# Reordering the first transfers of an eight-core decoder block, and moving the norm's scale from the multiply into the shift

## The chip, the cores and the metric

The kernel runs on all eight cores of one Trainium2 chip. Each core handles one sequence of the batch, and the cores exchange nothing. The metric is device time in microseconds (us) of the slowest core. Cores 0 to 3 are one die, 4 to 7 the other, and I call 0/1, 2/3, 4/5 and 6/7 pairs.

Most executions agree within a few tenths of a per cent. Some fall into a slow state: the cores of a whole die run at a lower clock, and the time is longer. All comparisons below use fast runs only.

## The reference, cut to what matters

```python
mod = silu(c) @ w_mod + b_mod                   # per sequence: shifts sh, scales sc, gates gt
h = rmsnorm(x, g1) * (1 + sc1) + sh1            # x: 4096 x 1024 per core, float32
x = x + 0.5 * gt1 * swiglu_ffn(h, w1_in, w1_out)
h = rmsnorm(x, gm) * (1 + sc2) + sh2            # mixing: convolution heads and a recurrence
x = x + gt2 * mix(h)
h = rmsnorm(x, g2) * (1 + sc3) + sh3
x = x + 0.5 * gt3 * swiglu_ffn(h, w2_in, w2_out)
y = rmsnorm(x, gf) * (1 + f_scale) + f_shift
```

Nothing can be multiplied until the scale `sc1` and the shift `sh1` exist, and each is a product of the conditioning vector with 4 MB of float32 weights.

## The kernel before

The program is built as a list of operations with dependences and priorities. A small scheduler in the builder then simulates the engines with assumed durations and fixes the order on each of them: the tensor engine (PE), the vector engine (DVE), the scalar engine (ACT), and two issuers of transfers, SP and POOL. Two facts matter later: an engine's order is static, and the assumed duration of a transfer is shorter than what it takes in a busy stretch (2.7 us assumed for a cast of weights, 9.5 to 13.0 measured for the first four in before).

```python
def load_slab(nm, r, cast, prio=None, after=()):     # 10 slots of 512 KB
    b = new(sl, f"{nm}{r}")
    if cast:                                         # first use: float32 in HBM -> bf16, issued by POOL
        dma("PL", lambda: b.ap, lambda: src, D_CAST, ..., slab=True, prio=prio, after=after)
        dma("SP", lambda: d.ap, lambda: b.ap, ...)   # and the bf16 copy is written back for later tiles
...
def mods(m, afters):                                 # one modulation vector: 8 slabs of 512 KB
    for q in range(8):
        b = new(sl, f"mod{m + q}")
        dma("SP", ..., slab=True, prio=P.prio)
        A("DVE", 1.3, f, [crow], [b, modr[m]], after=(afters[q],))   # multiply and sum, 1.2 us
...
P.prio = -24; mods(M_SC1, [None] * 8); gs_op(M_SC1, V_G1)   # scale: gs = g * (1 + sc)
P.prio = -20; mods(M_SH1, [None] * 8)                       # shift
...
def norm(xs, msc, msh, after=(), prio=None):
    r = stats(xs, after, prio)                       # squares (ACT), sums (DVE, PE), rsqrt (ACT)
    for f in range(8):
        stt(t_, xs[f], gs[msc], r, mult, mult)       # DVE: (x * gs) * r
        act(b, t_, Identity, bias=modv[msh])         # ACT: + shift, to bf16; DVE may take it
...
for pi, tiles in enumerate(pairs):                   # two tiles of 512 tokens share each weight slab
    xss = [load_x(x_dr, t, prio=(-22 if t == 0 else -15) if pi == 0 else lp, after=prev_in[...]) for t in tiles]
    hbs = [norm(xs, M_SC1, M_SH1, after=(last_in,), prio=300) for xs in xss]
    for j in range(FC):                              # 22 slabs of the input weights
        slab = load_slab("w1i", j, pi == 0)
        ops = ffn_in(slab, hbs, hids, j)             # both tiles: gate and up, 16 matmuls each
        if pi == 0 and j == 1:
            gt_anchor = ops[-1]
        if j >= 3:
            next_in.append(ops[-1])                  # the next pair's x loads follow these, one by one
    if pi == 0:
        mods(M_GT1, [gt_anchor] * 8)                 # the gate GT1: 8 more slabs
    ...                                              # output weights, then the next pair
```

The next pair's tiles 2 and 3 matter below: the chunks of their x load beside slabs 3 to 18 of the first pair.

## Time and profile before

| | before |
|---|---|
| timed runs | 2420.52, 2420.62 us, and 2465.01 (slow) |
| profiled execution, slowest core | 2431.0 us (core 1), 2432.64 us in all |
| PE busy | 2317.3 us, 95% of the span |
| first weight matmul | 66.40 us |

The busy time by stretches of the profiled core of before. Columns: the stretch, its length, busy us of each engine (with the number of instructions), the granted PE clock, the share of time in which the 16 DMA engines were busy, and what they moved.

```profile
core 1: us, PE busy (x) PEld busy (x) DVE busy (x) ACT busy (x) POOL busy (x), PEclk, DMA share, GB/s
0.00:45.00 45.00, 1.17 (x2) 0.21 (x2) 19.47 (x44) 14.06 (x20) 1.94 (x7) 1.00 0.96 259
45.00:70.00 25.00, 4.77 (x11) 1.56 (x12) 19.66 (x34) 11.16 (x17) 1.05 (x2) 1.00 1.02 286
70.00:90.00 20.00, 20.00 (x91) 8.96 (x90) 11.03 (x19) 6.69 (x10) 2.11 (x4) 1.00 0.54 168
90.00:200.00 110.00, 110.00 (x512) 49.88 (x510) 25.73 (x40) 19.12 (x32) 10.55 (x20) 1.00 1.03 209
200.00:300.00 100.00, 94.36 (x428) 42.19 (x427) 34.88 (x52) 24.82 (x40) 10.75 (x20) 0.97 0.70 199
...
```

Before 70 us PE does almost nothing while the DMA engines are full. From 70 to 90 us they are half idle, and from 90 to 200 us both PE and DMA are full.

The timeline of PE in before, ahead of its first weights and at tile 3. The brackets hold the idle time before a piece and what ended it.

```profile
49.24 0.59 PE L443 MATMUL ps<-sb_h,sb_ones 128*128 128x512 bf16 x1 [3.51 <-DVE sb_h L423]
66.40 4.00 PE L443 MATMUL ps<-sb_h,sb_slab 128*128 128x512 bf16 x9 [16.57 <-ACT sb_h L401]
...
227.77 0.38 PE L443 MATMUL ps<-sb_h,sb_ones 128*128 128x512 bf16 x1
233.78 0.59 PE L443 MATMUL ps<-sb_h,sb_ones 128*128 128x512 bf16 x1 [5.63 <-DVE sb_h L423]
```

Matmuls with `sb_ones` sum the squares for the norm; those with `sb_slab` are weight matmuls. The 5.63 us at 228 us is PE waiting for the squares of tile 3, whose x had not landed.

The two operations of the norm among the groups by form (busy us, mean ns of one):

```profile
L419 DVE SCALAR_TENSOR_TENSOR sb_c<-sb_c,sb_gs 128x512 f32<-128x512 f32 x256 | 173.5, 746 | 32.6 <-ACT sb_c L401 32.5
...
L401 ACT ACTIVATE sb_h<-sb_c,sb_modv 128x512 bf16<-128x512 f32 x160 | 105.1, 716 | 20.5 <-DVE sb_c L419 10.3 <-DVE sb_modv L423 9.6 <-issue 0.2
```

### The profile page before, as it was taken

How to read it: one execution, taken by the hardware profiler on the slowest of the kernel's cores; microseconds unless marked ns; L12 is line 12 of the kernel's file. 1: busy time of each engine (PE TensorE's matmuls, PEld its weight loads, DVE VectorE, ACT ScalarE, POOL GpSimd, SP SyncE). 2: the span in 40 equal slices, each digit the busy share in tenths (PEclk: the TensorE clock that was granted, in tenths of full speed). 3: DMA queues.
4: the chain of work that ended last, by engine and by line, in shares of the span. 5: the costliest groups of instructions: out<-in, count | busy, mean ns of one | idle time of the engine just before them, and what ended most of it. 6: DMA issues, size and time to landing. Idle time of an engine off the chain costs nothing.

```text
span 2431.0 us, 34520 instructions; the slowest of 8 cores (2409.5 to 2431.0 us)
## 1 busy us (share of the span) xinstructions
PE 2317.3 (95%) x11168; PEld 1093.3 (45%) x11168; DVE 1180.9 (49%) x1975; ACT 920.8 (38%) x1394; POOL 115.1 (5%) x221
## 2 busy tenths in 40 slices
PE   0999999999999999999899999999999999999996
PEld 0444444444444445454354454454454454454442
DVE  4513233523352337676285385484484574573322
ACT  2313111401130115556264364364364464473312
POOL 0100100010000000000000000000000000000000
PEclk9999999999999999999999999999999999999998
DMA  9899589768966755565976555555555555555551
GB/s 266 201 210 242 161 203 231 181 193 206 222 188 178 191 160 196 168 216 163 223 190 220 190 176 189 185 179 189 176 179 185 191 182 182 186 179 189 166 181 61
DMA packets 131711, 460.32 MB, mean 189 GB/s; under 512 B 16048, under 2 KB 16176, under 8 KB 130864
## 3 DMA queue, kind: packets, MB, share of 16 engines
q1 hardware_dynamic: 113184, 378.15, 48.8%
q0 software_dynamic: 18352, 79.97, 16.4%
q8 instruction: 94, 1.54, 0.3%
q14 instruction: 81, 0.66, 0.1%
HBM read 446.78 MB, written 79.69 MB: 217 GB/s over the span
## 4 chain that ended last, share of the span: by engine, by line
PE 84%; DMA 5%; SPq 4%; ACT 3%; issue 2%; DVE 2%; ACTq 0%; DVEq 0%; POOL 0%; POOLq 0%
PE ps L443 84%; SPq L450 4%; ACT sb_c L401 2%; DMA sb_c<-xmid 2%; DMA sb_c<-x 1%; DMA sb_slab<-wmod 1%; DMA sb_slab<-w2o 1%; DVE sb_c L734 0%; DVE sb_c L409 0%; ACT L401 0%; DVE sb_h L423 0%; ACT sb_h L401 0%; DVE sb_c L423 0%; DVE sb_c L419 0%; DVE sb_c L429 0%
## 5 line engine op out<-in xcount | busy, mean ns | idle before, releaser
L443 PE MATMUL ps<-sb_h,sb_slab 128*128 128x512 bf16 x9984 | 2176.7, 380 | 16.6 <-ACT sb_h L401 16.6
L443 PEld LDWEIGHTS ps<-sb_h,sb_slab 128*128 128x128 bf16 x9984 | 978.7, 98 | 1196.5 <-issue 28.0
L423 DVE TENSOR_TENSOR sb_h<-ps,sb_c 128x512 bf16<-128x512 f32 x352 | 240.7, 690 | 770.0 <-PE ps L443 728.3
L401 ACT ACTIVATE sb_c<-ps 128x512 f32<-128x512 f32 x400 | 237.7, 596 | 891.8 <-PE ps L443 891.4
L401 ACT ACTIVATE sb_c<-sb_c 128x512 f32<-128x512 f32 x332 | 204.4, 627 | 294.3 <-DVE sb_c L419 194.9
L401 ACT ACT_TABLE_LOAD x102 | 130.9, 1283 | 219.3 <-PE ps L443 195.9
L419 DVE SCALAR_TENSOR_TENSOR sb_c<-ps,sb_gth,sb_c 128x512 f32<-128x512 f32 x128 | 94.9, 749 | 216.6 <-PE ps L443 215.9
L423 DVE TENSOR_TENSOR sb_c<-sb_c 128x512 f32<-128x512 f32 x224 | 149.1, 687 | 88.3 <-ACT sb_c L401 85.8
L419 DVE SCALAR_TENSOR_TENSOR sb_c<-sb_c,sb_gs 128x512 f32<-128x512 f32 x256 | 173.5, 746 | 32.6 <-ACT sb_c L401 32.5
L443 PE MATMUL ps<-sb_ub,sb_slab 128*128 128x256 bf16 x1024 | 115.0, 273 | 4.9 <-DVE sb_c L409 4.4
L401 ACT ACTIVATE sb_h<-sb_c,sb_modv 128x512 bf16<-128x512 f32 x160 | 105.1, 716 | 20.5 <-DVE sb_c L419 10.3
L499 DVE SCALAR_TENSOR_TENSOR sb_slab<-sb_slab,sb_crow 128x1024 f32<-128x1024 f32 x88 | 107.0, 1217 | 11.9 <-DMA sb_slab<-wmod 11.3
L443 PEld LDWEIGHTS ps<-sb_ub,sb_slab 128*128 128x128 bf16 x1024 | 99.6, 98 | 21.9 <-issue 8.1
L443 PE MATMUL ps<-sb_h,sb_ones 128*128 128x512 bf16 x96 | 34.8, 391 | 71.6 <-DVE sb_h L423 71.0
L450 POOL DMA_DIRECT2D y<-sb_c x64 | 34.5, 540 | 1124.1 <-ACT sb_c L401 974.9
L423 DVE TENSOR_TENSOR sb_h<-sb_c 128x512 bf16<-128x512 f32 x96 | 65.3, 688 | 25.4 <-ACT sb_c L401 23.3
L419 DVE SCALAR_TENSOR_TENSOR sb_c<-sb_ux,sb_vecs,sb_c 128x512 f32<-128x512 f32 x96 | 69.5, 745 | 1.7
L419 DVE SCALAR_TENSOR_TENSOR sb_c<-ps,sb_modv,sb_c 128x512 f32<-128x512 f32 x64 | 47.9, 749 | 32.4 <-PE ps L443 32.4
L419 DVE SCALAR_TENSOR_TENSOR sb_ub<-sb_c,ps 64x256 bf16<-64x256 f32 x128 | 53.8, 420 | 15.1 <-PE ps L443 11.7
L450 POOL DMA_DIRECT2D xmid<-sb_c x64 | 34.8, 544 | 360.0 <-DVE sb_c L419 358.3
L401 ACT ACTIVATE sb_c<-sb_c,sb_lam 128x512 f32<-128x512 f32 x64 | 50.0, 821 | 0.5
L443 PEld LDWEIGHTS ps<-sb_h,sb_ones 128*128 128x128 bf16 x96 | 9.0, 98 | 88.8 <-issue 81.9
(51 smaller groups left out, 508.7 us busy)
## 6 DMA issues: line engine op xcount, KB each, us to landing
sb_slab<-b_w2i SPq DMA_DIRECT2D x176, 512.0 KB, 3.7
sb_slab<-wmod SPq DMA_DIRECT2D x88, 512.0 KB, 5.9
sb_slab<-b_w2o SPq DMA_DIRECT2D x84, 512.0 KB, 3.5
sb_slab<-b_w1i SPq DMA_DIRECT2D x66, 512.0 KB, 6.0
sb_slab<-b_win SPq DMA_DIRECT2D x64, 512.0 KB, 4.4
sb_slab<-b_dcw SPq DMA_DIRECT2D x64, 512.0 KB, 3.5
sb_slab<-b_w1o SPq DMA_DIRECT2D x36, 512.0 KB, 5.2
sb_c<-x SPq DMA_DIRECT2D x64, 256.0 KB, 10.7
```

Of the source, the lines that this page charges most:

```text
L401: return A("ACT", dur, lambda: (lambda o, i: (lambda h: [h.activation(out=o, in_=i, func=func, bias=bias, scale=scale)]))(out(), in_()), r ...
L419: return A("DVE", dur, lambda: (lambda o, a, b: (lambda h: [h.scalar_tensor_tensor(out=o, in0=a, scalar=scalar, in1=b, op0=op0, op1=op1)]) ...
L423: return A("DVE", dur, lambda: (lambda o, a, b: (lambda h: [h.tensor_tensor(out=o, in0=a, in1=b, op=op)]))(out(), in0(), in1()), reads, wr ...
L443: return [h.matmul(o, lhsT=l, rhs=r, start=(first and i == 0), stop=(last and i == n - 1)) for i, (l, r) in enumerate(pr)]
L450: lambda: (lambda o, i: (lambda h: [h.dma_start(out=o, in_=i)]))(out(), in_()),
L499: return lambda h: [h.scalar_tensor_tensor(out=w, in0=w, scalar=1.0, in1=crow.ap, op0=ALU.mult, op1=ALU.mult, accum_out=o)]
```

## The change

The intent: bring in first what is needed first. The order becomes x of tile 0, the 16 modulation slabs with the first two weight casts among them, then x of tile 1, then the other casts. The gate GT1 is put off until slab 8, the small `gates` matrix until the second pair. In the norm the DVE multiply becomes `x * r` alone, which needs no modulation and can run early; the scale joins the shift in the ACT operation. The first gate matmuls are split so that each waits for its own chunk.

```diff
-    stt(t_, xs[f], gs[msc], r, mult, mult)          # DVE
+    tt(t_, xs[f], r, mult)                          # DVE
-    act(b, t_, Identity, bias=modv[msh])
+    act(b, t_, Identity, bias=modv[msh], scale=gs[msc])    # the last norm likewise
...
+    if split:                                       # slab 0 only
+        for kc in range(8): mms(bg, [one matmul], [slab, hb[kc]], first=(kc == 0), last=(kc == 7))
...
+    if pi == 0:
+        xss = [load_x(x_dr, t, prio=-26 if t == 0 else -15, after=[None if t == 0 else sh1_last] * 8) for t in tiles]
+        hbs = [norm(xs, M_SC1, M_SH1, prio=-23 if t == 0 else 300) for t, xs in zip(tiles, xss)]
...
-    slab = load_slab("w1i", j, pi == 0)
+    slab = load_slab("w1i", j, pi == 0, sync=() if pi else (mod_ops[M_SH1 + 2 * j] if j < 2 else xss[-1][3 if j == 2 else 7].lw,),
+                     after=[xb.lw for xb in xss[-1]] if pi == 0 and j >= 2 else ())
-    if pi == 0 and j == 1:
+    if pi == 0 and j == 8:
         gt_anchor = ops[-1]
...
-    loads.sort(key=lambda o: use[o.writes[0]])
+    loads.sort(key=lambda o: (min(o.prio, 0), use[o.writes[0]]))
```

In words, `sync` makes cast 2 (the third) wait until chunk 3 of tile 1's x has landed, and the later ones until chunk 7 has.

More of the change, by code (lines that the diff above doesn't have):

```diff
@@ L420, in stt, with tt @@
                      reads, writes, prio=prio, after=after)
-        def tt(out, in0, in1, op, reads, writes, dur=0.69, prio=None):
-            return A("DVE", dur, lambda: (lambda o, a, b: (lambda h: [h.tensor_tensor(out=o, in0=a, in1=b, op=op)]))(out(), in0(), in1()), reads, writes, prio=prio)
+        def tt(out, in0, in1, op, reads, writes, dur=0.69, prio=None, after=()):
+            return A("DVE", dur, lambda: (lambda o, a, b: (lambda h: [h.tensor_tensor(out=o, in0=a, in1=b, op=op)]))(out(), in0(), in1()), reads, writes, prio=prio, after=after)
         def tsc(out, in0, s1, s2, op0, op1, reads, writes, dur=0.45):
@@ L457, in build_program, with load_slab @@
         slot_sem = lambda b, q="SP": (lambda: b.pool.sems[q][b.slot])
-        def load_slab(nm, r, cast, prio=None, after=()):
+        def load_slab(nm, r, cast, prio=None, after=(), sync=()):
             b = new(sl, f"{nm}{r}")
@@ L462, in load_slab @@
                 src = dr(w_src[nm], r)
-                dma("PL", lambda: b.ap, lambda: src, D_CAST, slot_sem(b, "PL"), [], [b], slab=True, prio=prio, after=after)
+                dma("PL", lambda: b.ap, lambda: src, D_CAST, slot_sem(b, "PL"), [], [b], slab=True, prio=prio, after=after, sync=sync)
                 d = scr[nm][r]
@@ L474, in build_program @@
         dma("SP", lambda: crow.ap, lambda: crow_d[:, :], D_SLAB, lambda: sem_c, [], [crow], prio=-30)
-        dma("PL", lambda: gates.ap, lambda: gates_d[:, :].rearrange("p (c n) -> p c n", c=8), 1.0, lambda: sem_g, [], [gates], prio=5000, after=(None,))
         sem_v, sem_c, sem_g = newsem("s_vecs"), newsem("s_crow"), newsem("s_gates")
@@ L486, in build_program @@
         act(k_(crow.ap), k_(crow.ap), AF.Silu, [crow], [crow], dur=1.1, tset=(SILU,))
+        mod_ops = {}
         def mods(m, afters):
@@ L500, in f @@
                                                              op1=ALU.mult, accum_out=o)]
-                A("DVE", 1.3, f, [crow], [b, modr[m]], after=(afters[q],))
+                last = A("DVE", 1.3, f, [crow], [b, modr[m]], after=(afters[q],))
+                mod_ops[m + q] = last
             tt(k_(modv[m].ap), k_(modr[m].ap), k_(V[:, V_BMOD + m:V_BMOD + m + 8]), ALU.add, [modr[m], vecs], [modv[m]], dur=0.17)
+            return last
         def gs_op(m, g):
@@ L513, in build_program @@
         P.prio = -20
-        mods(M_SH1, [None] * 8)
+        sh1_last = mods(M_SH1, [None] * 8)
         P.prio = 4000
@@ L557, in norm, with ffn_in @@
                 t_ = new(p2, "nt")
-                stt(lambda t_=t_: t_.ap, lambda f=f: xs[f].ap, gs[msc].ap[:, f:f + 1], lambda: r.ap, ALU.mult, ALU.mult,
-                    [xs[f], r, gs[msc]], [t_], after=after, prio=prio)
+                tt(lambda t_=t_: t_.ap, lambda f=f: xs[f].ap, lambda: r.ap, ALU.mult, [xs[f], r], [t_], prio=prio, after=after)
                 b = new(p1, "hb")
                 o, i = (lambda b=b: b.ap), (lambda t_=t_: t_.ap)
-                act(o, i, AF.Identity, [t_, modv[msh]], [b], dur=0.7, bias=modv[msh].ap[:, f:f + 1], prio=prio,
-                    alt=v_ts(o, i, modv[msh].ap[:, f:f + 1], ALU.add))
+                act(o, i, AF.Identity, [t_, modv[msh], gs[msc]], [b], dur=0.72, bias=modv[msh].ap[:, f:f + 1],
+                    scale=gs[msc].ap[:, f:f + 1], prio=prio,
+                    alt=v_ts(o, i, gs[msc].ap[:, f:f + 1], ALU.mult, modv[msh].ap[:, f:f + 1], ALU.add))
                 hb.append(b)
             return hb
-        def ffn_in(slab, hbs, hids, j):
+        def ffn_in(slab, hbs, hids, j, split=False):
             w = lambda kc, o: (lambda: slab.ap[:, kc * 256 + o:kc * 256 + o + 128])
@@ L572, in ffn_in @@
                 bg = new(ps, "g")
-                mms(bg, [(w(kc, 0), lambda kc=kc, hb=hb: hb[kc].ap) for kc in range(8)], [slab] + hb)
+                if split:
+                    for kc in range(8):
+                        mms(bg, [(w(kc, 0), lambda kc=kc, hb=hb: hb[kc].ap)], [slab, hb[kc]], first=(kc == 0), last=(kc == 7))
+                else:
+                    mms(bg, [(w(kc, 0), lambda kc=kc, hb=hb: hb[kc].ap) for kc in range(8)], [slab] + hb)
                 bu = new(ps, "u")
@@ L615, in build_program @@
             lp = -25 if pi == 0 else 400 + pi * 100
-            xss = [load_x(x_dr, t, prio=(-22 if t == 0 else -15) if pi == 0 else lp, after=prev_in[8 * (t % 2):8 * (t % 2) + 8]) for t in tiles]
-            hbs = [norm(xs, M_SC1, M_SH1, after=(last_in,), prio=300) for xs in xss]
+            if pi == 0:
+                xss = [load_x(x_dr, t, prio=-26 if t == 0 else -15, after=[None if t == 0 else sh1_last] * 8) for t in tiles]
+                hbs = [norm(xs, M_SC1, M_SH1, prio=-23 if t == 0 else 300) for t, xs in zip(tiles, xss)]
+            else:
+                xss = [load_x(x_dr, t, prio=lp, after=prev_in[8 * (t % 2):8 * (t % 2) + 8]) for t in tiles]
+                hbs = [norm(xs, M_SC1, M_SH1, after=(last_in,), prio=300) for xs in xss]
             hids = [[] for _ in tiles]
@@ L620, in build_program @@
             for j in range(FC):
-                slab = load_slab("w1i", j, pi == 0)
-                ops = ffn_in(slab, hbs, hids, j)
+                slab = load_slab("w1i", j, pi == 0, sync=() if pi else (mod_ops[M_SH1 + 2 * j] if j < 2 else xss[-1][3 if j == 2 else 7].lw,),
+                                 after=[xb.lw for xb in xss[-1]] if pi == 0 and j >= 2 else ())
+                ops = ffn_in(slab, hbs, hids, j, split=(j == 0))
                 anchors.append((pi, ops[-1]))
-                if pi == 0 and j == 1:
+                if pi == 0 and j == 8:
                     gt_anchor = ops[-1]
@@ L644, in build_program @@
             mid = [mid[0]]
+        dma("PL", lambda: gates.ap, lambda: gates_d[:, :].rearrange("p (c n) -> p c n", c=8), 1.0, lambda: sem_g, [], [gates], prio=5000, sync=(mid[0],))
         psem = [VB(ap=None) for _ in range(8)]
@@ L819, in mix_ffn2 @@
                 b = xs[f]
-                stt(lambda b=b: b.ap, lambda b=b: b.ap, gs[M_SCF].ap[:, f:f + 1], lambda r=r: r.ap, ALU.mult, ALU.mult, [r, gs[M_SCF]], [b])
+                tt(lambda b=b: b.ap, lambda b=b: b.ap, lambda r=r: r.ap, ALU.mult, [r], [b])
                 o = lambda b=b: b.ap
-                act(o, o, AF.Identity, [modv[M_SHF]], [b], dur=0.7, bias=modv[M_SHF].ap[:, f:f + 1],
-                    alt=v_ts(o, o, modv[M_SHF].ap[:, f:f + 1], ALU.add))
+                act(o, o, AF.Identity, [modv[M_SHF], gs[M_SCF]], [b], dur=0.72, bias=modv[M_SHF].ap[:, f:f + 1],
+                    scale=gs[M_SCF].ap[:, f:f + 1],
+                    alt=v_ts(o, o, gs[M_SCF].ap[:, f:f + 1], ALU.mult, modv[M_SHF].ap[:, f:f + 1], ALU.add))
                 d = VB(ap=dr(y_d, t * 8 + f))
```

## The prediction

> **What bounds the kernel.** PE: busy 2317.3 of 2431.0 us on the profiled (slowest) core. Of its 114 idle us, the busy time by stretches puts 65 ahead of the first weight matmul (66.40 us), 5.6 between 200 and 300 us, about 20 in the mixing stages and 22 after 2300 us. What can be won at once is in the first 66 us, and there the DMA engines are the limit: busy share 0.92 to 1.02, 262 to 278 GB/s.
>
> **What fills those 66 us (timeline, transfers by tile).** The first weight matmul needs x of tile 0 (2 MB), 16 modulation slabs (8 MB) and one weight cast. Before or among them stand x of tile 1 (2 MB, landing from 33 to 48 us), gates, six of the eight slabs of the gate GT1 and two more casts. The last shift slab lands at 58.7 us; the sums end at 60.6, and eight normalised chunks come from ACT 0.66 us apart, so PE, which waits for all eight, starts at 66.40 ("ACT sb_h" wait, 16.6 us).
>
> **What the change does.**
> 1. Order: x of tile 0, the 16 slabs, w1i0 and w1i1 behind shift slabs 0 and 2, then x of tile 1. The second shift slab landed at 32.9 us with the same bytes ahead of it as after the change. The six others take 10 us (48.5 to 58.7 in the trace), one cast with them about 3 us[...]. So the shift slabs are done at about 45 us.
> 2. Norm: the DVE multiply no longer needs the modulation, so it runs before; with the first gate matmuls split, PE starts one ACT op after the shift, at 47 to 48 us. It then follows ACT for eight chunks, cold: the first 11 matmuls start 0.43 us apart, later ones 0.21 ([...]the trace shows 4.6 us).
> 3. x of tile 1 lands at about 54 us, its norm needs 5 us; by then PE has tile 0 of two slabs. A stall of 0 to 4 us is likely. I value the start at 13 to 16 us.
> 4. Norm cost: DVE 746 to about 688 ns (groups by form), 256 times; ACT 716 to about 810 ns: [...]the trace agrees (821 ns with two, 710 with one). Neither engine is critical (49%, 38%), so 0; the last norm gets up to 1 us longer.
>
> **What is given back.** From 90 to 220 us the DMA share is 1.0 (write-backs land after 26 us). Only some 9 us were idle there (70 to 90 us, shares 0.50 and 0.59), because GT1 held the slots. GT1's loads now fall into the saturated stretch. PE's stall at 228 us for x of tile 3 (5.6 us; 0 to 6 on other cores) is a DMA arrival and can come only some 9 us earlier, so it should grow to 8 to 12 us. Net 9 to 15 us.
>
> **Predicted:** 2409 us, 2400 to 2418. Faster by over 2%: 0.02; within: 0.96; slower: 0.02.
>
> **What would show it.** First weight matmul at 45 to 50 us; shift sum at 45 to 48; little DMA idle from 70 to 90; the stats stall near 215 us longer than 5.6 us; ACT norm ops near 810 ns; PE busy unchanged.
>
> **What would make it wrong.** Casts starved behind SP's queue; GT1 slabs late and holding DVE in order, so that PE starves around slab 9; the static order reshuffled later; less stall than I fear at tile 3.

Its sum: the start at 13 to 16 us, a stall at tile 3 that grows from 5.6 to 8 to 12 us, net 9 to 15, and from 2420.6 us that gives 2409. The "about 3 us" for one cast is an estimate of mine; point 1 of the review near the end sets it against packet times of the trace. "Cold" is measured in before: the first 11 distances from one start of a weight matmul to the next are 0.38 to 0.43 us, 4.6 us together, then one of 0.25 and after it 0.21 to 0.22. The 821 and 710 ns are ACT operations of before on tiles of the same shape, with scale and bias both read from a tile (`sb_lam`) and with the bias alone (`sb_cst`).

## The result, and the profile after

| | before | after |
|---|---|---|
| median of fast runs | 2420.52 us | 2416.45 us |
| all runs | 2465.01, 2420.52, 2420.62, 2418.84 | 2414.38, 2877.22 (slow), 2416.45, 2416.78 |
| ratio of fast runs | | 0.9983, 95% interval 0.996 to 1.0006 |
| first weight matmul, profiled core | 66.40 us | 43.22 us |

A ratio is the mean time of one kernel's fast runs over that of the other's of the same rounds, so it is not quite the ratio of the medians. The change saved about 4 us, within the interval of no change at all. The prediction had said 2409 with a range of 2400 to 2418: the time lies in the range, but the saving is a third of the 11.6 us that I had named.

The stretches of after, on its slowest core:

```profile
core 4: us, PE busy (x) PEld busy (x) DVE busy (x) ACT busy (x) POOL busy (x), PEclk, DMA share, GB/s
0.00:45.00 45.00, 2.94 (x7) 0.97 (x8) 33.27 (x71) 13.14 (x18) 1.41 (x6) 1.00 0.95 281
45.00:70.00 25.00, 17.23 (x65) 6.89 (x65) 12.79 (x20) 15.62 (x22) 3.70 (x7) 0.86 1.01 224
70.00:90.00 20.00, 19.89 (x92) 9.07 (x93) 4.06 (x6) 3.58 (x6) 0.54 (x1) 1.00 1.04 216
90.00:200.00 110.00, 109.47 (x501) 49.90 (x510) 31.88 (x50) 19.10 (x32) 10.54 (x20) 1.00 0.99 220
200.00:300.00 100.00, 94.14 (x421) 42.38 (x429) 34.59 (x53) 26.34 (x40) 11.19 (x21) 0.97 0.68 206
...
```

PE does 17 us of work before 70 us in place of 5, and the idle DMA time from 70 to 90 us is gone (0.54 to 1.04). Both are as intended. But the granted clock from 45 to 70 us is 0.86: something dropped it.

The timeline of PE in after, in the same two places:

```profile
43.22 9.19 PE L443 MATMUL ps<-sb_h,sb_slab 128*128 128x512 bf16 x32 [26.70 <-ACT sb_h L401]
52.26 0.38 PE L443 MATMUL ps<-sb_h,sb_ones 128*128 128x512 bf16 x1
55.71 0.38 PE L443 MATMUL ps<-sb_h,sb_ones 128*128 128x512 bf16 x1 [3.08 <-DVE sb_h L423]
60.72 9.63 PE L443 MATMUL ps<-sb_h,sb_slab 128*128 128x512 bf16 x34 [4.63 <-DMA sb_slab<-w1i]
...
214.80 0.38 PE L443 MATMUL ps<-sb_h,sb_ones 128*128 128x512 bf16 x1
220.39 0.59 PE L443 MATMUL ps<-sb_h,sb_ones 128*128 128x512 bf16 x1 [5.21 <-DVE sb_h L423]
```

PE starts 23.2 us earlier. Then it runs out of work: 3.08 us for tile 1's squares and 4.63 us for the third cast. The wait at tile 3 comes 13.0 us earlier and is still there. The POOL timeline of after shows why the third cast is late:

```profile
49.28 0.53 POOL L450 DMA_DIRECT2D sb_slab<-w1i  x1 [12.95 <-DMA sb_c<-x]
53.51 3.17 POOL L450 DMA_DIRECT2D sb_slab<-w1i  x6 [3.69 <-DMA sb_c<-x]
```

POOL sat 12.95 us until chunk 3 of x had landed, issued the cast at 49.28, and PE got going on it at 60.72, 11.4 us later. The trace has the cast itself landing 11.3 us after its issue, and the two before it, issued at 33.19 and 35.79 us, after 9.3 and 11.9; the DMA share was 0.95 up to 45 us and 1.01 from 45 to 70. The shortest of these casts in before landed after 8.3 us; it was issued at 84.94 us, and the DMA share from 80 to 90 us was 0.59. How much of the 11 us the full DMA engines make up no run shows.

The norm's operations in after, again by form:

```profile
L423 DVE TENSOR_TENSOR sb_c<-sb_c 128x512 f32<-128x512 f32 x480 | 307.8, 689 | 115.4 <-ACT sb_c L401 112.6
...
L401 ACT ACTIVATE sb_h<-sb_c,sb_modv,sb_gs 128x512 bf16<-128x512 f32 x151 | 108.9, 801 | 36.7 <-DVE sb_modv L423 22.9 <-DVE sb_c L423 13.8
```

The multiply fell from 746 to 689 ns, the ACT operation rose from 716 to 801 ns. So reading the scale from a tile as well cost ACT 85 ns.

### How far each core is at a given time

Spans of whole runs mix everything, so I use a finer measure, worked out from the trace: the time of PE's n-th weight load, as a mean of the eight cores. Both kernels do the same loads, so the same n from 200 on is the same amount of work done.

| n-th weight load | before | after | difference |
|---|---|---|---|
| 200 | 110.4 us | 97.6 us | -12.8 |
| 710 (just ahead of tile 3's gap) | 220.4 | 207.6 | -12.8 |
| 800 (just after it) | 245.8 | 233.7 | -12.0 |
| 1200 | 332.1 | 320.1 | -12.0 |
| 11168, the last | 2399.9 | 2386.2 | -13.8 |

In this pair of traces the change keeps 12 to 14 us. The timed runs say 4. The traced execution of before took 2432.64 us, 12 us more than its timed runs; that of after took 2414.38 us, 2 us less than its own. So this pair of traces can't stand for the timed runs, and a second pair was wanted. The spans of one pair show how far cores of one execution differ, before:

```profile
core 2: 2418.5 us, clock 0.994
core 3: 2409.5 us, clock 0.995
```

In after the same two took 2401.0 and 2409.8 us. One core of a pair is about 9 us slower than the other in nearly every execution, now this one, now that. I compare means over cores for that reason.

### The profile page after: what moved, and what is told of

It is laid out like the page before. It is cut to its first block, busy times and chain, and to the rows that moved or that the text cites. A ratio compares the mean times of both kernels' runs of the same rounds, so it can differ in the third digit from the quotient of the medians.

```text
span 2412.5 us, 34309 instructions; the slowest of 8 cores (2400.9 to 2412.5 us)
## 1 busy us (share of the span) xinstructions
PE 2306.1 (96%) x10957; PEld 1093.0 (45%) x11168; DVE 1180.2 (49%) x1995; ACT 928.1 (38%) x1378; POOL 115.2 (5%) x221
## 4 chain that ended last, share of the span: by engine, by line
PE 84%; DMA 7%; ACT 3%; issue 3%; DVE 2%; SPq 1%; POOL 0%; ACTq 0%; DVEq 0%; POOLq 0%
PE ps L443 84%; DMA sb_c<-x 3%; ACT sb_c L401 2%; DMA sb_c<-xmid 2%; DMA sb_slab<-w1o 1%; SPq L450 1%; DMA sb_slab<-w2o 1%; DVE sb_c L423 1%; DMA sb_slab<-wmod 1%; DMA sb_slab<-w1i 0%; DVE sb_c L747 0%; ACT L401 0%; DVE sb_c L409 0%; DVE sb_h L423 0%; DVE sb_c L419 0%
## 5 line engine op out<-in xcount | busy, mean ns | idle before, releaser
L423 DVE TENSOR_TENSOR sb_c<-sb_c 128x512 f32<-128x512 f32 x480 | 307.8, 689 | 115.4 <-ACT sb_c L401 112.6
L401 ACT ACTIVATE sb_c<-sb_c 128x512 f32<-128x512 f32 x322 | 197.8, 627 | 271.4 <-DVE sb_c L419 192.4
L401 ACT ACTIVATE sb_h<-sb_c,sb_modv,sb_gs 128x512 bf16<-128x512 f32 x151 | 108.9, 801 | 36.7 <-DVE sb_modv L423 22.9
L423 DVE TENSOR_TENSOR sb_h<-sb_c 128x512 bf16<-128x512 f32 x96 | 65.5, 690 | 22.9 <-ACT sb_c L401 21.0
L419 DVE SCALAR_TENSOR_TENSOR sb_ub<-sb_c,ps 64x256 bf16<-64x256 f32 x128 | 53.8, 420 | 15.1 <-PE ps L443 11.6
L409 DVE TENSOR_SCALAR sb_c<-ps,sb_vecs 64x256 f32<-64x256 f32 x85 | 40.7, 484 | 8.9 <-ACT sb_c L401 4.7
L401 ACT ACTIVATE sb_c<-ps,sb_bah 128x512 f32<-128x512 f32 x64 | 37.8, 702 | 10.8 <-PE ps L443 10.8
```

What stands on the lines that cost most here:

```text
L401: return A("ACT", dur, lambda: (lambda o, i: (lambda h: [h.activation(out=o, in_=i, func=func, bias=bias, scale=scale)]))(out(), in_()), r ...
L409: f = lambda: (lambda o, a: (lambda h: [h.tensor_scalar(out=o, in0=a, scalar1=s1, scalar2=s2, op0=op0, op1=op1)]))(out(), in0())
L419: return A("DVE", dur, lambda: (lambda o, a, b: (lambda h: [h.scalar_tensor_tensor(out=o, in0=a, scalar=scalar, in1=b, op0=op0, op1=op1)]) ...
L423: return A("DVE", dur, lambda: (lambda o, a, b: (lambda h: [h.tensor_tensor(out=o, in0=a, in1=b, op=op)]))(out(), in0(), in1()), reads, wr ...
```

## The experiments

Sixteen kernels ran, in four groups of four on four chips. In the texts, single letters name the theories as each text tells. All kernels but one (`gt1_small`) gave correct results. No ratio below is as much as 2% from 1, so the verdicts are "same" or "unclear"; what follows reads smaller differences. Each verdict has its own runs of before on the same chip. "Mean core" is the mean span of all cores of the fast runs; "slowest core" is the mean reported time.

### Group 1, chip A: both kernels again, and each half of the change alone

`before_again` and `after_again` are the two kernels unchanged.

> The kernel before, unchanged, as a control. The progress of PE (time of its n-th weight load) says the change gained 12.0 us on the mean core at 300 us and 13.8 us at the end, but the timed runs say 4 us. Theory A: the profile of before was an unlucky execution (2432.6 against 2420.6 us timed), so that a second one has its mean core near 2412 us, not 2420, and its slowest near 2420; the loss lies in the first 70 us. Theory B: the profile was typical of the mean core, and only the slowest core of the eight, which is the metric, hides the gain: mean core again near 2420, slowest again near 2430 in the profile. Ratio to before 1.000 in either.

> The change, unchanged, with five rounds for a tight interval. Theory A (before's profile unlucky): ratio 0.998, mean core 5 us below before. Theory B (slowest core hides it): mean core 12 to 14 us below before_again in the same rounds, slowest core 4 us below. First weight matmul at 43 to 45 us, then stalls of 3 and 4.6 us.

`order_only` takes the change and puts the norm back:

```diff
-    tt(t_, xs[f], r, mult)
-    act(b, t_, Identity, bias=modv[msh], scale=gs[msc])
+    stt(t_, xs[f], gs[msc], r, mult, mult)
+    act(b, t_, Identity, bias=modv[msh])
```

> The change with the old norm (DVE multiplies by gain and 1/rms, ACT adds the shift). Theory C (the new norm costs nothing after the start): first weight matmul 1 to 2 us later than in the change, total within 2 us of the change. Theory D (the new norm's ACT work or its reshuffled static order costs in the mixing stages): total 3 us or more below the change.

`norm_only` takes before and puts in the same two operations the other way round, with nothing moved in the order.

> Before with the new norm alone. Theory C: within 2 us of before (first weight matmul at about 65 us instead of 66.4, since the multiply runs before the modulation). Theory D: 3 us or more slower than before. ACT's norm op goes from 716 to about 810 ns, DVE's multiply from 746 to 688 ns.

| chip A | slowest core | mean core | ratio [95%] | load 200 | load 710 | load 1200 |
|---|---|---|---|---|---|---|
| before | 2431.5 us | 2418.8 us | | | | |
| before_again | 2432.0 | 2419.2 | 1.0001 [0.9984, 1.0018] | 109.4 us | 219.5 us | 327.3 us |
| after_again | 2425.1 | 2414.0 | 0.9972 [0.9959, 0.9986] | 97.7 | 207.8 | 321.1 |
| order_only | 2427.8 | 2414.3 | 0.9984 [0.9969, 0.9999] | 98.9 | 209.0 | 323.3 |
| norm_only | 2428.7 | 2416.0 | 0.9985 [0.9972, 0.9998] | 105.9 | 216.0 | 325.2 |

What follows. First, the start repeats: -11.7 us at load 200. Second, **the trace of before changed**. Its gap at tile 3 was 4.0 us in the first profile and 0.9 us here. (I give gaps as PE's idle time in pieces over 0.5 us, as a mean of the cores; the texts count from one weight load to the next, which is some 0.4 us more.) On core 0 of `before_again`:

```profile
232.32 0.38 PE L443 MATMUL ps<-sb_h,sb_ones 128*128 128x512 bf16 x1 [1.54 <-DVE sb_h L423]
```

The gap of after was 4.5 us and is 3.8. So after's advantage falls from 11.7 us at load 710 to 7.1 at load 800, just behind the gap, and 6.2 at load 1200. The 4.6 us lost at tile 3 are, roughly, a gap that is 2.9 us longer and the half clock behind it: by the clock records it lost 2.4 us of the mean core in `after_again` and 0.2 in `before_again`. In the first pair the advantage fell by 0.8 only because that execution of before had a long gap of its own. At the last load the traces of this chip leave 1.2 us (2396.7 against 2397.9), where the first pair had 13.8. Of the 5.0 us lost after load 1200, the clock records put 1.8 down to more time at 0.81 in `after_again` (short stretches, see the end of this part) and 1.1 to more at half clock; the rest stays open. Neither theory hit whole: A foretold the gain of the timed mean core (5 us; it was 4.8), B the spans of `before_again` (2420 and 2430; they were 2418 and 2433 us in its profile).

Third, on the slowest core order alone saves 3.7 us and the norm alone 2.8, and both together 6.4, as if the halves added up. On the mean core they do not: 4.5, 2.8 and 4.8 us. What the norm adds to the new order is therefore not shown. By itself it saves time, more than expected (within 2 us). In `norm_only` PE started its weights at 61.7 us as a mean of the cores, 3.8 us before `before_again` (65.5), and kept 3.5 us at load 200. The trace says how: most of the multiplies were done before the shift came, so DVE was free and did four of the first eight shift operations. On core 0 the last of the eight chunks was ready 3.0 us after the shift, in place of 5.5 with all eight on ACT. The shift itself came 1.5 us earlier as a mean of the cores.

### Group 2, chip B: why PE starves twice

One theory put the early gap down to the third cast being held too long; `third_early` issues it behind the fifth shift slab instead of behind x of tile 1. For the gap at tile 3 the rivals were the order of issue and the amount of data: `x_early` loads x of tiles 2 and 3 two slabs earlier, `gt1_small` loads 1/16 of each GT1 slab (3.9 MB less, and a wrong result; its relative error was 0.24). `after_b` is the change once more.

```diff
 # third_early
-    sync=(mod_ops[M_SH1 + 2 * j] if j < 2 else xss[-1][3 if j == 2 else 7].lw,), after=... j >= 2
+    sync=(mod_ops[M_SH1 + 2 * j] if j < 3 else xss[-1][7].lw,), after=... j >= 3
 # x_early
-    if j >= 3:
+    if j >= 1:
         next_in.append(ops[-1])
 # gt1_small
+    n = 64 if m == M_GT1 else 1024
-    dma("SP", b.ap, src, ...)
+    dma("SP", b.ap[:, 0:n], src[:, 0:n], ...)
```

> The change once more, as the partner of the three runs beside it. 5 to 9 us below before (slowest core), 5 us on the mean core. Two early PE gaps of 3.3 and 4.4 us on the mean core at 52 and 56 us, one of 4 to 5 us near 215 us, and about 10 us more at half clock than before.

> The change, but the third weight cast no longer waits for four chunks of x of tile 1: it goes behind shift slab 4, as the first two go behind slabs 0 and 2. Theory E (the hold made PE wait for the third cast, 4.4 us, and the two gaps together cost one more fall to half clock): the gap at 56 us goes, PE then waits once for tile 1's sums, the cold stretch at 60 us is gone or shorter, 200th weight load 3 to 6 us earlier. Theory F (DMA time is only moved): x of tile 1 lands about 3 us later, the gap moves there, 200th weight load within 1.5 us of the change.

> The change, but the loads of x for tiles 2 and 3 are issued two weight slabs (about 14 us) earlier. Theory G (the gap near 215 us is x of tile 3 arriving behind write-backs and casts in a full DMA system): the gap of 4 to 5 us goes and with it the fall to half clock after it, 3 to 6 us less at the 800th weight load. Rival H (it is not those loads, or PE then starves for a cast instead): gap stays or appears elsewhere before 240 us, total within 2 us of the change.

> The change, but only 64 of the 1024 columns of each of GT1's eight slabs are loaded (wrong result on purpose; 3.9 MB or about 12 us of DMA time less between 60 and 200 us). My prediction said DMA time is conserved there and GT1's loads in the full stretch feed the gap near 215 us: then the gap goes. Rival: the gap stays at 4 us or more, because the wait is set by the order of issue on SP, which waits for casts before write-backs, not by the amount of data.

(The 14 us in `x_early` and the 12 us here are estimates: two slabs are 64 matmuls, 13.8 us at the 0.2158 us between matmul starts in before, and 3.9 MB take 12.1 us at the 321 GB/s that before moved from 10 to 20 us.)

| chip B | fast runs | slowest core | ratio [95%] |
|---|---|---|---|
| before | 5 of 11 | 2426.2 us | |
| after_b | 5 of 7 | 2437.6 | 1.0047 [0.9974, 1.012] |
| third_early | 2 of 8 | 2450.0 | 1.0098 [1.0067, 1.0129] |
| x_early | 5 of 6 | 2430.7 | 1.0018 [0.9955, 1.0082] |
| gt1_small | 2 of 4 | 2441.6 | none |

On this chip the change was not faster at all. The reason is in the spans of `after_b`, here of die 0:

```profile
core 0: 2437.9 us, clock 0.980
core 1: 2429.2 us, clock 0.981
core 2: 2409.4 us, clock 0.992
core 3: 2417.3 us, clock 0.992
```

One pair is 20 us behind the next at a lower clock. The stretches of core 0 and of core 2 of that execution say where:

```profile
45.00:68.00 23.00, 17.03 (x58) 6.52 (x57) 13.11 (x22) 15.11 (x22) 3.70 (x7) 0.85 1.02 219
68.00:230.00 162.00, 162.00 (x620) 67.17 (x618) 36.65 (x58) 24.35 (x41) 11.08 (x21) 0.81 0.95 211
230.00:400.00 170.00, 170.00 (x790) 77.07 (x788) 60.79 (x96) 39.65 (x62) 15.23 (x29) 1.00 0.78 190
```

```profile
45.00:68.00 23.00, 17.06 (x57) 6.64 (x57) 13.03 (x22) 16.30 (x23) 3.70 (x7) 0.85 1.03 232
68.00:230.00 162.00, 154.27 (x697) 69.91 (x710) 51.22 (x81) 37.05 (x61) 12.70 (x24) 0.98 1.00 230
230.00:400.00 170.00, 169.16 (x773) 77.08 (x788) 54.06 (x85) 29.95 (x47) 14.10 (x27) 1.00 0.76 199
```

From about 69 to 230 us the pair 0/1 ran at 0.81. It did 618 weight loads in that stretch where core 2 did 710. A stretch of 161 to 162 us at 0.81, in both cores of a pair at once, comes back below; I count it by the mean clock of a whole run, since a pair so hit shows less than 0.984 on both cores.

The gaps themselves I compare on cores that were not hit. `third_early` missed (its profile fell in the slow state, so I read the four cores of its undisturbed die): load 200 came at 100.6 us, against 97.6 on the six cores of `after_b` that were not hit. PE on core 4 of `third_early`:

```profile
58.98 0.38 PE L443 MATMUL ps<-sb_h,sb_ones 128*128 128x512 bf16 x1 [2.15 <-DVE sb_h L423]
66.83 13.54 PE L443 MATMUL ps<-sb_h,sb_slab 128*128 128x512 bf16 x55 [7.48 <-DMA sb_slab<-w1i]
```

and on core 4 of `after_b`:

```profile
57.18 0.58 PE L443 MATMUL ps<-sb_h,sb_ones 128*128 128x512 bf16 x1 [2.77 <-DVE sb_h L423]
60.00 20.38 PE L443 MATMUL ps<-sb_h,sb_slab 128*128 128x512 bf16 x84 [2.23 <-DMA sb_slab<-w1i]
```

The third cast came in time, and the static order then put the *fourth* slab of tile 0 ahead of tile 1. That cast still waited for all of x. PE stood for it 7.48 us, although the first chunk of tile 1 was ready at 63.8 us. The scheduler believes that a cast takes 2.7 us, and plans by that.

`x_early` hit (its edit moves the loads of later pairs of tiles too): on cores 2 to 7, which no 0.81 stretch touched in either profile, the mean gap at tile 3 fell from 6.3 to 2.3 us, and load 1200 came at 317.6 in place of 322.0 us. On core 2 of `x_early` the wait had shrunk to 3.26 us:

```profile
222.72 0.38 PE L443 MATMUL ps<-sb_h,sb_ones 128*128 128x512 bf16 x1 [3.26 <-DVE sb_h L423]
```

On the six cores of `gt1_small` that were not hit, the gap was 3.8 us and load 1200 came at 318.7 us, with 3.9 MB less moved. A gap of 3.8 us is not below what other executions of the change show (3.8 in `after_again`, 4.2 in `after_d`). Core 0 of `gt1_small`, 90 to 150 and 150 to 200 us:

```profile
90.00:150.00 60.00, 60.00 (x280) 27.20 (x278) 22.12 (x36) 10.15 (x17) 6.86 (x13) 1.00 0.75 172
150.00:200.00 50.00, 50.00 (x234) 22.63 (x232) 9.75 (x15) 8.88 (x15) 3.69 (x7) 1.00 1.03 212
```

The DMA engines had free time before 150 us (0.75, against 0.96 on core 2 of `after_b`) and were full after it, with the gap left. That free time was no use to x of tiles 2 and 3, because its chunks are issued one per slab, as PE gets on. So earlier issue shortens the gap. What the amount of data is worth stays open: by the gap it is worth less than the issue, but in timed runs the pairs that were not hit took the same in both, 2406.8 us in `x_early` (16 pairs) and 2406.5 in `gt1_small` (6 pairs), against 2412.1 in `after_b`.

### Group 3, chip C: the clock, and repeats

In the profile of after, the clock records show half clock for 6.8 to 10.2 us from about 57 us on all cores, around the second early gap, and for 3.4 to 6.8 us again at the gap at tile 3, on seven of the eight cores. In the profiles of before and after each such record ahead of 2300 us lasts 3.41, 6.83 or 10.24 us; whether a gap is followed by one does not go by its length alone (last section). `warm` keeps PE busy in the early gaps with 28 matmuls whose result is not used. `best` joins `x_early` and `third_early`, with an assumed 9.0 us for the fourth cast, so that the planner puts tile 1 first. `after_c` and `x_early_b` are repeats.

```diff
 # warm
+    if pi == 0 and j == 1:
+        warm(12, hbs[0][0], ops[0])          # 12 matmuls behind tile 0's second slab
+        warm(16, hbs[0][0], stat_ops[3])     # 16 behind tile 1's sums
 # best: x_early, third_early, and
-    dma("PL", ..., D_CAST, ...)
+    dma("PL", ..., 9.0 if late else D_CAST, ...)     # late: cast 3 of the first pair
```

> The change as the partner of the three runs beside it. Early gaps 3.3 and 4.4 us on the mean undisturbed core, 4 to 7 us near 215 us; PE falls to half clock for 6.8 us at about 57 us and again at about 219 us. 200th weight load at 97.5 us.

> Repeat of x_early, whose timed runs were disturbed. On undisturbed cores it was 4.5 us ahead of the change at the 800th weight load. If that is real, the slowest core is 3 to 5 us below the change in the same rounds; if the later stages give it back, within 1.5 us.

> The change with 28 idle matmuls (results never read) in the two early gaps: 12 before tile 1's sums, 16 before the third weight slab. Theory W (the gaps cost twice: idle time, then 6.8 us at half clock after them): no half-clock stretch at 57 us, the 200th weight load 2.5 to 3.5 us earlier, total 2 to 3.5 us less; and if falling to half clock is what brings on the 0.81 stretches of some core pairs that start 5 to 10 us later, none starts near 68 us. Rival: 200th weight load within 1 us, since PE then only waits longer for ACT's chunks or casts.

> x_early, plus the third cast behind shift slab 4, plus a longer assumed time for the fourth cast in the scheduler's model so that PE's static order takes tile 1 before the fourth slab (in third_early PE stood 8 us for that slab while tile 1 was ready). Expect one early gap of 5 to 6 us in place of 7.7, the gap near 215 us at most 3 us; 200th weight load 1 to 3 us before the change, total 4 to 7 us below the change. If DMA time is only moved, the 200th weight load is level with the change and the total as x_early.

| chip C | fast runs | slowest core | ratio [95%] | pairs at 0.81 for 161 us |
|---|---|---|---|---|
| before | 7 of 11 | 2425.3 us | | 0 of 28 |
| after_c | 4 of 6 | 2444.4 | 1.0091 [1.0074, 1.0108] | 9 of 16 |
| x_early_b | 3 of 7 | 2431.4 | 1.0028 [0.9975, 1.0081] | 2 of 12 |
| warm | 3 of 6 | 2429.0 | 1.0018 [0.9959, 1.0077] | 2 of 12 |
| best | 5 of 6 | 2418.4 | 0.9974 [0.996, 0.9988] | 0 of 20 |

`x_early_b` repeats the gain: load 1200 at 316.5 us on its cores that were not hit, against 321.0 of `after_c`.

`warm` removed the fall at 57 us. Its count of loads runs 28 ahead; with 6.0 us added for them (28 times 0.2158 us, the mean distance of matmul starts on the profiled core of before from 100 to 200 us), load 200 came at 96.2 us, 2.3 earlier than the 98.4 on cores 2 to 7 of `after_c`. But at load 1200 it was 320.8 against 321.0: the gap at tile 3 was 6.2 us, against 5.0 on those cores of `after_c`. The time won ahead of this wait for data was lost at the wait. The total, expected 2 to 3.5 us lower, was not: the pairs that were not hit took 2412.8 us, against 2410.1 in `after_c`.

`best` missed its first aim: it closed neither early gap (2.2 and 4.6 us), and its load 200 came at 100.8 us, 2.3 later than in `after_c`, where 1 to 3 earlier was expected. It shortened the gap at tile 3 to 2.7 us, and it beats before on this chip. By pairs that were not hit it lies behind `x_early_b` (2409.6 against 2406.8 us); in the timed runs it comes out ahead because none of its pairs was hit.

### Group 4, chip D: the best version, and a gap put into before

`warm_x` joins `warm` with x loaded three slabs earlier (`j >= 0`). `before_gap` tests whether a fall to half clock, by itself, brings on the 161 us at 0.81: it puts a gap of about 7 us into before at slab 9, with a chain of five DVE operations and one matmul that waits for them. `best_again` and `after_d` are repeats.

```diff
 # before_gap
+    if pi == 0 and j == 9:
+        for i in range(5):
+            A("DVE", 0.01, ...junk = junk * crow..., prio=-60)     # 6.5 us in all
+        mms(gb, [(ones, junkb)], [junkb, ones], prio=-60)           # PE waits for it
```

> The change as the partner. On a chip of the kind seen twice: in about half of its runs one core pair or more with a mean clock near 0.98 instead of 0.99, slowest core 0.5 to 0.9% above before. On a chip of the kind of the first two: no such pair, 0.2 to 0.3% below before.

> warm (28 idle matmuls in the early gaps) with x of tiles 2 and 3 issued three slabs earlier[...]. Theory K (a return from half clock brings on the 0.81 stretch): no half-clock stretch between 45 and 300 us, no pair near 0.98, slowest core 8 to 11 us below before. Rival L (the 0.81 stretch belongs to the earlier or denser load on the chip, not to the falls): pairs near 0.98 as often as in the change, on the same chip.

> The kernel before with a chain of five DVE ops (about 7 us, result unused) that PE waits for after the tenth slab of tile 0, near 134 us: one PE gap of 5 to 6 us and one fall to half clock, nothing else of the change. Theory K: pairs near 0.98 appear in some runs, as in the change, and a caught one begins 3 to 5 us after the return; without one, 6 to 9 us slower than before (gap plus half of 6.8 us). Rival L: no such pair in any run.

> Repeat of best: one fall to half clock at 62 us, none at 219 us. It had no pair near 0.98 in 22. Theory K says it can have some, as one return is left; if none again, then more than the return is needed (in best all PE work after the return is spread by ACT's chunks). Slowest core 5 to 8 us below before on any chip without such a pair.

| chip D | fast runs | slowest core | mean core | ratio [95%] |
|---|---|---|---|---|
| before | 8 of 11 | 2423.4 us | 2413.9 us | |
| after_d | 5 of 7 | 2419.6 | 2410.4 | 0.9984 [0.997, 0.9998] |
| warm_x | 4 of 8 | 2411.7 | 2402.9 | 0.9954 [0.9927, 0.9981] |
| best_again | 5 of 6 | 2415.4 | 2407.0 | 0.9967 [0.9952, 0.9982] |
| before_gap | 5 of 6 | 2430.5 | 2423.0 | 1.0029 [1.0016, 1.0042] |

PE on core 4 of `warm_x` (L539 are the added matmuls; the piece of 144.77 us has no break, and no idle time stands before the sums at tile 3):

```profile
56.16 3.61 PE L539 MATMUL ps<-sb_h,sb_ones 128*128 128x512 bf16 x16
60.29 4.05 PE L443 MATMUL ps<-sb_h,sb_slab 128*128 128x512 bf16 x18 [0.51 <-DMA sb_slab<-w1i]
65.03 144.77 PE L443 MATMUL ps<-sb_h,sb_slab 128*128 128x512 bf16 x670 [0.70 <-DMA sb_slab<-w1i]
...
213.31 0.59 PE L443 MATMUL ps<-sb_h,sb_ones 128*128 128x512 bf16 x2
```

The clock records show one fall to half clock between 45 and 300 us, on one core alone. Load 1200, counted as for `warm`, came at 312.5 us against 319.8 of `after_d`: 7.3 us more than the change gains, and the timed mean core agrees (2402.9 against 2410.4). With both waits gone the time stays won. `warm_x` beats before by 11.7 us and the change by 7.9, the largest gain of all versions.

PE on core 0 of `before_gap`:

```profile
142.44 0.58 PE L445 MATMUL ps<-sb_junkb,sb_ones 128*128 128x512 bf16 x1 [6.47 <-DVE sb_junkb L633]
```

The gap and the half clock after it cost 9.1 us of the mean core and 7.1 of the slowest. That is 2.6 us more than the gap of 6.5 alone (half of the 6.83 us at half clock would be 3.4), so the fall of the clock is lost time on top of the gap. The 0.81 stretch did not follow. But on this chip it followed on no kernel, the change included (0 of 20 pairs in `after_d`), so the run can't rule it out.

### What all four chips say of the change

Taking only the pairs that were not hit by the 161 us stretch, in fast runs:

| mean core, us | before | after | difference | pairs of after hit | pairs of before hit |
|---|---|---|---|---|---|
| chip A | 2418.8 | 2414.0 | -4.8 | 0 of 20 | 0 of 36 |
| chip B | 2416.6 | 2412.1 | -4.5 | 3 of 20 | 0 of 20 |
| chip C | 2416.1 | 2410.1 | -6.0 | 9 of 16 | 0 of 28 |
| chip D | 2413.9 | 2410.4 | -3.5 | 0 of 20 | 0 of 32 |

The gain of the change is 3.5 to 6.0 us on all chips. By the same count `x_early` gained 9.8 and 9.3 us, `best` 6.5 and 6.9, `warm_x` 11.0, `gt1_small` 10.1, `third_early` 5.9 and `warm` 3.3.

On two chips a second effect takes more than the gain away again. Shorter stretches at 0.81 show in other traces: of 4 to 8 us on die 1 of chip A, in before too (`before_again`), and of 15.2 us in three traces of the changed order (`after_again`, `order_only`, `after_d`). The long one I never saw with before in a fast run. But the count leaves out slow runs. One slow run of before on chip C (2460.24 us) has one pair at 0.981 and 0.980 and its other cores at 0.993 to 0.995, so by this count before can be hit as well. And runs in which both pairs of one die were hit, and no other, count as slow: `x_early_b` 2441.08 and 2443.65 us, `warm` 2446.66, `third_early` 2451.72.

I leave the cause of the long stretch open. For a link with the half clock speaks the timing: in all five profiled fast executions that caught it (`after_b`, `after_c`, `x_early`, `x_early_b`, `gt1_small`) it began 3 to 5 us after both cores of the pair had returned from half clock, for instance 64.3 and 64.6, then 68.8 and 69.1 us. It also began at 68.0 to 69.1 us in all five, so a fixed moment would fit them too; but in the slow profile of `third_early` it began on all four cores of die 0 at 232 us, about 4 us after both cores of each pair had returned from the fall at tile 3. Against a link with the fall at 57 us alone speaks `warm`, which had no such fall and still 2 of 12 pairs hit; it kept the fall after tile 3, and no profile caught a pair of it in the act. `best` had a fall near 60 us and 0 of 20.

## Why the prediction was right or wrong

1. **"First weight matmul at 45 to 50 us; shift sum at 45 to 48": right in kind, and early.** They came at 43.2 and 42.0 us. (The 3 us for one cast were an estimate. The trace of before has 407 ns as the mean of the 415 cast packets of 4 KB before 66 us; a cast has 128 of them, and spread over the 16 DMA engines they take 3.3 us.)
2. **"A stall of 0 to 4 us is likely. I value the start at 13 to 16 us": wrong in size.** The stall was two gaps with a sum of 7.7 us on the profiled core and a mean of 7.3 us over the cores, and the start was worth 11.7 to 12.8 us. I had counted the wait for x of tile 1, and overlooked that the third cast was held behind that same x and needs another 11 us to land. I had counted a slow stretch of PE only once, at the start; after these gaps the records show half clock from about 57 us, for 6.8 to 10.2 us. `warm` puts the fall and the gaps it fills at 2.3 us.
3. **"Little DMA idle from 70 to 90": right**, 0.54 to 1.04.
4. **Norm cost, "so 0": right for the cost, wrong for the whole.** The operations measured 689 and 801 ns, predicted 688 and 810. I had folded the norm's gain into the start. Alone it is worth 2.8 us of the mean core, the order alone 4.5, and both together 4.8.
5. **"PE's stall at 228 us for x of tile 3 (5.6 us; 0 to 6 on other cores) is a DMA arrival and can come only some 9 us earlier, so it should grow to 8 to 12 us": this step failed.** In after the gap was 5.2 us on the profiled core, and it came 13 us earlier, not 9. I took the base from one execution of before, whose span was 12 us longer than its timed runs. A second execution had a mean gap of 0.9 us in place of 4.0, against 3.8 of after there. The reason I gave, that data which must arrive can't arrive sooner, holds in part: the gap does grow, by 2.9 us from a near-empty base. But x can arrive sooner: issued two slabs earlier, with nothing less to move, it brought the gap from 6.3 to 2.3 us. The loads of x are paced by PE's own progress, which I had overlooked; how much the full DMA engines add stays open (`gt1_small`). And the growth costs half clock too, which I had left out.
6. **"Net 9 to 15 us": the sum that was wrong.** Its first term, the start, measured 11.7 to 12.8 us in place of 13 to 16. Its second, what tile 3 takes back, measured 4.6 us on chip A. My 5.6 growing to 8 to 12 implied 2.4 to 6.4, so that size was hit by luck: base and end were both wrong, and the half clock was missing. These two leave 7.1 us at load 800 and not 9 to 15. Timed runs gain 3.5 to 6.0 us of the mean core, so a further 1 to 4 us go later. The traces of chip A lose even 5.9 us after load 800; the clock records put about 4 us of that down to more 0.81 stretches and more half clock, and the rest stays open. That 2416 us lay inside 2400 to 2418 owes more to the width of the range than to the sum.
7. **"PE busy unchanged": not testable to this precision.** It fell from 2317.3 to 2306.1 us, but 211 of the 11168 matmul records are missing in after.
8. **Not foreseen at all:** the 161 us at 0.81, which turns a gain into a loss on two of the four chips of the experiments. It did not shape the first result: no pair there was hit.

## What to carry to other kernels

An earlier start is worth only what the next wait lets through: here 12 us won at the start shrank to 7 at the next late transfer, and a version that also removed that wait kept 11. When one profile is the base of a prediction, compare its span with the timed runs first, and read a stall from more than one execution before building on it. A transfer held behind another cost the landing time of both: POOL stood 12.95 us for x, and the third cast then took 11.3 to land. And a planner that assumed 2.7 us for such a cast put the wrong work first (PE stood 7.48 us in `third_early`).

## What the traces show of the clock and of one gap

- All eight cores run dense matmuls, with a mean clock of 0.993 to 0.996 in the first profile of before. In the five fast profiles that caught it, the 0.81 came on one pair of a die, the other pair staying near 0.99 as a mean, and it ended after 161 to 162 us with PE still busy (core 0 of `after_b`: 162.00 of 162.00 us from 68 to 230 us, 170.00 of 170.00 from there to 400). (By mean clocks, two fast runs of `after_c` had both pairs of die 0 hit.)
- A PE gap has a price: in `before_gap` one of 6.5 us with the half clock that follows cost 9.1 us of the mean core. The length of the gap alone does not decide whether half clock follows, though. At tile 3, gaps of 2.2 and 2.5 us (`norm_only`, cores 5 and 4) and of 2.7 to 2.8 us (before, cores 7, 4 and 0) were followed by 3.41 us at half clock; gaps of 3.5 to 3.7 us (`best`, cores 4, 3 and 1) were not.
- Two executions of one kernel can differ in a single gap: the one at tile 3 of before had a mean of 4.0 us in one profile and 0.9 us in the next.
